# Latent attention heads of a diffusion backbone: scores turned to keys by queries, in a phase of their own

## The chip, the cores and the metric

The kernel runs on one core of one Trainium2 chip. The metric is the device time of one execution in microseconds (us); less is better. The core has a matmul engine (TensorE, PE in the profile, with its weight loads as PEld), a vector engine (DVE), a scalar engine (ACT), a general engine (POOL) and a queue that issues the transfers (SP). Each runs its own instructions strictly in the order in which they were written, and waits on semaphores for the others.

## The reference

A backbone of two layers works on 1024 latent tokens and 256 context tokens of width 1024. Layer 0 has two groups of attention heads side by side: four differential heads and eight latent heads (multi-head latent attention). Layer 1 is an mLSTM with a neighbourhood attention, and is not touched here. What the change touches is the attention of the latent heads:

```python
def softmax_attention(q, k, v, scale):
    def one(qb):
        s = jnp.einsum('bhqd,bhkd->bhqk', qb, k).astype(F32) * scale
        p = jax.nn.softmax(s, axis=-1).astype(v.dtype)
        return jnp.einsum('bhqk,bhkd->bhqd', p, v)
    return blocked_queries(one, q)
...
    oa = rms_norm(diff_attention(q1, q2, k1, k2, vd, lam), subln_g) * (1.0 - lam_init)
    ob = softmax_attention(qm, km, vm, MLA_SCALE)
    y = jnp.concatenate([from_heads(oa), from_heads(ob)], axis=-1) * jax.nn.silu(gate)
```

A latent head has 96 rows of queries and keys (64 plus 32 rotated ones) and 64 columns of values. All is in fp32. A latent query sees 1280 keys (1024 latent and 256 context tokens), a context query only the 256 context keys. A softmax is the same whatever is subtracted from all the scores of one query, so long as the exponentials stay in range.

## The kernel before

The kernel goes through stages: the conditioning and the input projection of layer 0 (to about 460 us in the profile), the attention of layer 0 (460 to 1006 us), its output projection, and layer 1. Only the attention stage concerns us.

**Units and tiles.** The stage has eight units: four `Differential` heads and four `Latent` units of two heads each. A unit works on ten tiles of 128 queries: eight latent ones with 1280 keys, and two context ones with 256. An fp32 operand is kept as two fp32r numbers, a high and a low part, so that one product of scores takes several quick passes: two in a differential head (L568, L569), three in a latent head (L720 high by high, L721 high by low, L722 low by high).

**One latent tile, one head** (`Latent.plan`): `cut` writes the scores, 128 queries by 1280 keys, in pieces of 512, 512 and 256 columns into one of two wide score buffers in PSUM (`s`, three banks each). `top` (DVE, L1151) takes the highest score of each query, `exps` (ACT, L1158) takes the exponentials and their sum, `inverse` (L733) and `scale` (POOL, L737) divide by the sum. Then `turned` transposes the ten 128 by 128 pieces on PE (L1175), since the product with the values needs the keys on the partitions; `moves` copies them out of the two small PSUM buffers `tp` (L518, on ACT or DVE), and `values` (L745) multiplies them with the values, the two heads of a unit on the two halves of the output's partitions. The values, the probabilities and the transposes are plain fp32; each such product stands as two instructions in the profile.

**A differential tile** is alike, with two scores, two exponentials and one combination of both (L588, DVE), ten transposes and ten products with the values (L599).

**Order.** A planner (`Plan`) takes all tasks of the stage with a cost each, and always emits next the task that could start earliest by these costs. So the order on each engine is fixed before the run. It was given the units in two streams: the tiles of the differential heads and the tiles of the latent units, one of the first to one of the second (`RATE = 1.0`), the differential ones eight tiles ahead (`LEAD = 8`). So the first differential head runs nearly alone, and then both kinds alternate.

**Loads.** Each stream has one set of buffers for queries, keys and values (pool `a0` for the differential units, `a1` for the latent ones). The loads of a stream's next unit (`load_scores`, `load_values`; L543 to L545 and L690 to L692, by the SP queue) can start only when its last scores have been taken by PE. A latent unit loads two times 2.0 MB of queries and keys (480 + 320 + 160 KB, high and low, for two heads), and 640 KB each of values and of the gate.

Of the kernel before, what the change touches and what calls it, by code (L numbers as in the profile page):

```python
# [49 lines left out]
NP = 5  # L50
# [87 lines left out]
def hybrid_kernel(ctx, tc, t, out, dbg=None):  # L138
# [352 lines left out]
    def on_vector(n):  # L491
        return 0.07 + n / 960
# [38 lines left out]
    class Differential(Unit):  # L531
        def __init__(self, h):
            self.h = h
            self.q, self.kh, self.kl = [None, None], [None, None], [None, None]
# [22 lines left out]
        def plan(self, tt):  # L557
# [53 lines left out]
            for b in range(2):  # L611
                last = None
                for n0, nn in key_cuts(w):
                    last = plan.add("P", 2 * nn / 2400, cut(b, n0, nn), [last or self.ready[b]], ["s"] if n0 == 0 else [],
                                    [f"dk{b}"] if tt == TILES - 1 and n0 + nn == w else [], rank=RD)
# [16 lines left out]
        def finish(self, t0, n, last):  # L632
# [42 lines left out]
            last = plan.add("V", 0.06 + on_vector(n * P), gated, [last], ["yd"], ["tp"] + (["dv"] if end else []))  # L675
# [4 lines left out]
    class Latent(Unit):  # L680
        def __init__(self, p):
            self.p, self.yy = p, {}
            self.qh, self.ql, self.kh, self.kl = [[None, None] for _ in range(4)]

        def load_scores(self, pool, a):
            p = self.p
            o = pool.tile([P, 4, NT], FR, name=f"o{a}")
            self.qh[a], self.ql[a], self.kh[a], self.kl[a] = [o[0:96, i, :] for i in range(4)]
            for i, (q, k) in enumerate(((self.qh, self.kh), (self.ql, self.kl))):
                dma(out=q[a].bitcast(F32), in_=s_mq[i][2 * p + a])  # L690
# [10 lines left out]
        def order(self):  # L701
            return [(tt, a) for tt in range(TILES) for a in range(2)]

        def plan(self, tt, a):
            k0, w = keys_of(tt)
            nch = w // P
            if a == 0:
                self.pair = []
            pair = self.pair
            x = {}  # L710
            pair.append(x)
            qsl = slice(tt * P, (tt + 1) * P)

            def cut(n0, nn):
                def emit(_):
                    if n0 == 0:
                        x["s"] = taken("s")
                    s = x["s"]
                    ks = slice(k0 * P + n0, k0 * P + n0 + nn)
                    T.matmul(s[:, n0:n0 + nn], self.qh[a][:, qsl], self.kh[a][:, ks], start=True, stop=False)  # L720
                    T.matmul(s[:, n0:n0 + nn], self.qh[a][:, qsl], self.kl[a][:, ks], start=False, stop=False)  # L721
                    T.matmul(s[:, n0:n0 + nn], self.ql[a][:, qsl], self.kh[a][:, ks], start=False, stop=True)  # L722
                return emit

            def top(_):
                x["m"] = highest(x["s"], w)

            def exps(_):
                x["p"], x["z"] = exponentials(x["s"], x["m"], w)
                given("s", x["s"])  # L730

            def inverse(_):
                V.reciprocal(out=x["z"], in_=x["z"])  # L733

            def scale(cs):
                def emit(_):
                    G.tensor_scalar(out=x["p"][:, cs], in0=x["p"][:, cs], scalar1=x["z"], scalar2=1.0,  # L737
                                    op0=ALU.mult, op1=ALU.mult)
                return emit

            def values(_):
                x["o"] = o = taken("tp")
                for c in range(nch):
                    for b in range(2):
                        T.matmul(o[64 * b:64 * b + 64, :P], self.v[:, k0 + c, b * 64:(b + 1) * 64], pair[b]["pt"][:, c, :],  # L745
                                 start=c == 0, stop=c == nch - 1)
                for y in pair:
                    given("pt", y["pt"])

            def gated(_):  # L750
                i = tt % 2
                if i == 0:
                    self.yy[tt // 2] = at.tile([P, 256], F32, name="yy", bufs=2)
                V.tensor_tensor(out=self.yy[tt // 2][:, i * P:(i + 1) * P], in0=x["o"][:, :P], in1=self.gate[:, qsl],
                                op=ALU.mult)
                given("tp", x["o"])

            def store(_):
                dma(out=s_y[4 + self.p, :, (tt - 1) * P:(tt + 1) * P], in_=self.yy[tt // 2])

            last = None
            for n0, nn in key_cuts(w):
                last = plan.add("P", 3 * nn / 2400, cut(n0, nn), [last or self.ready[a]], ["s"] if n0 == 0 else [],
                                [f"mk{a}"] if tt == TILES - 1 and n0 + nn == w else [], rank=RM)
            last = plan.add("V", on_vector(w), top, [last], rank=RANK)
            last = plan.add("A", on_scalar(w) + 0.1, exps, [last], ["p"], ["s"], rank=RANK)
            last = plan.add("V", 0.08, inverse, [last], rank=R1)
            done = [plan.add("G", on_pool(nn), scale(slice(n0, n0 + nn)), [last]) for n0, nn in pieces(w)]
            x["moved"] = turned(lambda: x["p"], x, w, done)
            if a:  # L770
                o = plan.add("P", 0.27 * nch, values, pair[0]["moved"] + x["moved"] + self.ready[2:], ["tp"], ["pt", "pt"])
# [1593 lines left out]
```

## Time and profile before

| | |
|---|---|
| median of 3 runs | 1916.51 us (1907.38 to 1920.92) |
| the profiled execution | 1925.9 us, its span 1923.8 us |
| mean granted PE clock of the span | 0.974 |
| PE busy | 1811.8 us, 94% of the span |
| DVE, ACT, POOL busy | 1083.7, 782.2, 527.2 us |
| attention stage | 460.6 to 1006.5 us, 546 us |

How to read it: a group is one line of the code on one engine with one form of operands; it shows how often it ran, its busy time together and the mean of one. Matmuls are pipelined, so the length of one is longer than the distance to the next; what a matmul costs PE is the distance between two starts. "PEclk" is the share of full speed at which the chip let PE run.

### The profile page before, as it was taken

Reading aid. Unit: us, or ns where it says so; the run is one execution under the profiler, and the core shown is the slowest. Engines: PE = TensorE matmul, PEld = TensorE weight load, DVE = VectorE, ACT = ScalarE, POOL = GpSimd, SP = SyncE. Lnnn points to the kernel's source line nnn. Section 1 sums busy time; section 2 is a strip of 40 time slices with the busy share of each in tenths; the row PEclk is TensorE's granted clock in tenths of the full one; section 3 lists DMA queues with packets and bytes.
Section 4 is the critical chain, followed back from the end, with each engine's and each line's share of the span. In section 5 each row is a group of like instructions: output and inputs, shape, how many; then the busy total and the mean of one; then the engine's idle time right before and its main releaser. Section 6 shows DMA issues by size and latency. Waiting matters only on the chain.

```text
span 1923.8 us, 33069 instructions
## 1 busy us (share of the span) xinstructions
PE 1811.8 (94%) x12493; PEld 1579.9 (82%) x12493; DVE 1083.7 (56%) x2273; ACT 782.2 (41%) x1622; POOL 527.2 (27%) x650
## 2 busy tenths in 40 slices
PE   7999999999989989899999989999998998998898
PEld 5898999887878778688878879788898877887786
DVE  2754124322867667567757863765766124667756
ACT  2311013433756656556653222324543223444521
POOL 1433124210133322223454422220111002223444
PEclk9999999999999999899999999999999999999999
DMA  9766524668330741830856432225442366677642
GB/s 285 238 206 203 169 76 129 184 192 200 74 86 15 163 107 22 167 92 13 215 165 224 142 138 77 78 74 194 152 136 76 107 191 173 167 188 194 180 159 88
DMA packets 242755, 276.17 MB, mean 144 GB/s; under 512 B 25170, under 2 KB 203294, under 8 KB 242598
## 3 DMA queue, kind: packets, MB, share of 16 engines
q1 hardware_dynamic: 242598, 274.07, 49.6%
q8 instruction: 99, 1.62, 0.3%
q14 instruction: 58, 0.48, 0.1%
HBM read 193.14 MB, written 87.16 MB: 146 GB/s over the span
## 4 chain that ended last, share of the span: by engine, by line
PE 62%; DMA 9%; DVE 5%; issue 2%; ACT 2%; SPq 2%; POOL 0%; DVEq 0%; POOLq 0%; ACTq 0%
PE mm L390 7%; PE mm L392 7%; PE mm L391 7%; PE tp L1175 4%; PE tp L745 4%; DMA o<-s_qk 3%; PE tp L599 3%; PE mm L1778 3%; PE mm L1779 3%; PE mm L1780 3%; PE s L569 2%; DMA o<-s_kr 2%; PE s L568 2%; PE s L720 2%; PE tp L2211 2%
## 5 line engine op out<-in xcount | busy, mean ns | idle before, releaser
L1151 DVE TENSOR_REDUCE nm<-s 128x1 f32<-128x1280 f32 (+1 forms) x160 | 202.9, 1274 | 105.1 <-PE s L569 71.5
L1158 ACT ACTIVATE p<-s,nm 128x1280 f32<-128x1280 f32 (+1 forms) x160 | 185.6, 1160 | 44.4 <-DVE nm L1151 31.7
L737 POOL TENSOR_SCALAR p<-p,zs 128x512 f32<-128x512 f32 (+1 forms) x208 | 128.4, 634 | 270.3 <-DVE zs L733 235.2
L518 ACT COPY pt<-tp 128x256 f32<-128x256 f32 x346 | 118.7, 375 | 113.2 <-PE tp L1175 106.5
L1175 PE MATMUL tp<-cst,p 128*128 128x128 f32 x1008 | 157.0, 279 | 3.8 <-DVE zs L733 1.4
L347 POOL TENSOR_TENSOR wlo<-raw,whi 128x1024 fp32r<-128x1024 f32 (+2 forms) x40 | 96.7, 2417 | 213.5 <-ACT whi L339 213.4
L1175 PEld LDWEIGHTS tp<-cst,p 128*128 128x128 f32 x1008 | 120.9, 143 | 34.3 <-issue 8.9
L390 PE MATMUL mm<-whi,hhi 128*128 128x256 f32 (+1 forms) x496 | 147.6, 298 | 0.5 <-DVE z L975 0.5
L392 PE MATMUL mm<-whi,hlo 128*128 128x256 f32 (+1 forms) x496 | 146.6, 296 | 0.2 <-DVE hlo L290 0.2
L391 PE MATMUL mm<-wlo,hhi 128*128 128x256 f32 (+1 forms) x496 | 146.4, 295 | 0.0
L339 ACT CAST whi<-raw 128x1024 fp32r<-128x1024 f32 (+2 forms) x54 | 55.9, 1036 | 178.4 <-DMA raw<-in_ev_w_in_dram 72.7
L2168 POOL TENSOR_SCALAR np<-np,nrz 128x640 f32<-128x640 f32 x64 | 52.1, 818 | 235.1 <-DVE nrz L2165 221.0
L568 PE MATMUL s<-o 128*128 128x512 f32 (+1 forms) x208 | 86.7, 419 | 16.4 <-DMA o<-s_qk 8.6
L518 DVE COPY pt<-tp 128x256 f32<-128x256 f32 x158 | 64.2, 421 | 66.8 <-ACT pt L518 57.8
L390 PEld LDWEIGHTS mm<-whi,hhi 128*128 128x128 f32 x496 | 94.6, 191 | 2.8 <-issue 1.7
L392 PEld LDWEIGHTS mm<-whi,hlo 128*128 128x128 f32 x496 | 94.5, 191 | 0.5 <-DVE hlo L290 0.4
L391 PEld LDWEIGHTS mm<-wlo,hhi 128*128 128x128 f32 x496 | 94.7, 191 | 0.2
L720 PE MATMUL s<-o 96*128 96x512 f32 (+1 forms) x208 | 87.8, 422 | 1.4 <-ACT p L1158 1.4
L599 PE MATMUL tp<-v,pt 128*128 128x128 f32 x672 | 85.1, 282 | 0.2
L745 PE MATMUL tp<-pt,v 128*64 128x128 f32 x1344 | 83.8, 279 | 0.4 <-ACT pt L518 0.2
L599 PEld LDWEIGHTS tp<-v,pt 128*128 128x128 f32 x672 | 80.7, 196 | 4.1 <-ACT pt L518 1.9
L721 PE MATMUL s<-o 96*128 96x512 f32 (+1 forms) x208 | 74.8, 360 | 9.4 <-DMA o<-s_kr 9.4
(451 smaller groups left out, 5049.2 us busy)
## 6 DMA issues: line engine op xcount, KB each, us to landing
adaw<-in_ada_w_dram SPq DMA_DIRECT2D x16, 1024.0 KB
raw<-in_od_w_in_dram SPq DMA_DIRECT2D x32, 512.0 KB
o<-s_qk SPq DMA_DIRECT2D x48, 320.0 KB
raw<-in_ev_w_in_dram SPq DMA_DIRECT2D x18, 512.0 KB
bt<-s_bt SPq DMA_DIRECT2D x16, 576.0 KB
adaw<-in_ada_w_dram SPq DMA_DIRECT2D x16, 512.0 KB
o<-s_mq SPq DMA_DIRECT2D x16, 480.0 KB
s_gate<-e SPq DMA_DIRECT2D x24, 256.0 KB
```

Source lines behind the costliest of these rows:

```text
L390: T.matmul(ps, ahi(k), bhi(k), start=k == k0, stop=False)
L391: T.matmul(ps, ahi(k), blo(k), start=False, stop=False)
L392: T.matmul(ps, alo(k), bhi(k), start=False, stop=k == nk - 1)
L518: copy_by(eng)(out=dst()[:, c0:c1, :], in_=bank()[:, c0 * P:c1 * P].rearrange("p (c q) -> p c q", q=P))
L568: T.matmul(s[:, n0:n0 + nn], ql, self.kh[b][:, ks], start=True, stop=False)
L599: T.matmul(o[:, :P], x["pt"][:, c, :], self.v[:, k0 + c, :], start=c == 0, stop=c == nch - 1)
L720: T.matmul(s[:, n0:n0 + nn], self.qh[a][:, qsl], self.kh[a][:, ks], start=True, stop=False)
L737: G.tensor_scalar(out=x["p"][:, cs], in0=x["p"][:, cs], scalar1=x["z"], scalar2=1.0, op0=ALU.mult, op1=ALU.mult)
L745: T.matmul(o[64 * b:64 * b + 64, :P], self.v[:, k0 + c, b * 64:(b + 1) * 64], pair[b]["pt"][:, c, :], start=c == 0, stop=c == nch - 1)
L1151: V.tensor_reduce(out=nm, in_=s[:, :w], axis=AX.X, op=ALU.max, negate=True)
L1158: S.activation(out=p[:, :w], in_=s[:, :w], func=AF.Exp, bias=nm, accum_out=z)
L1175: T.transpose(ps[:, c * P:(c + 1) * P], p()[:, (c0 + c) * P:(c0 + c + 1) * P], ident)
```

## The change

The differential heads come first, all four, and then the four latent units in a phase of their own (the two streams, `RATE` and `LEAD` are not used any more). The units alternate between the two sets of buffers (`place`), so a unit's loads can start when the unit before the last one has ended.

A latent unit works on groups of 512, 512 and 256 queries (`TG`), in two steps:

- `shifts`: for each head and each tile of 128 queries only the leading pass (high by high) is taken, into the wide buffer `s` (`rough`, L716); DVE takes the highest of each query with its sign turned (`top`, L724), four of them are transposed into one row (`turn`, L732), and ACT writes it as a 97th row under the low part of the queries (`row`, L737). The high part of the keys has a 97th row of ones, which POOL writes at each load (L692). The group after the current one has its shifts taken between the blocks of the current one.
- `scores`: one block is 128 keys by 512 queries (`block`, L763 to L765): three passes again, of which the third has 97 rows and so subtracts the shift. `exps` (L779) takes the exponential, which already has the keys on the partitions. `values` (L799) takes it as the moving operand, 64 rows of output for each head by 512 queries, for five chunks of keys at a time. The sums of the exponentials are added up chunk by chunk (`total`, L790, on DVE or POOL), one product with ones sums them over the partitions (`sums`, L807), `inverse` (L814) takes the reciprocal in two halves, and `gated` and `scaled` (L821, L825) apply the gate and the reciprocal.

One of the two wide buffers `s` is handed over to the blocks as three buffers `st` of one bank each (`banks`); the shifts have the other one alone. The ten wide tiles `p` and `pt` now hold the ten chunks of one group.

```diff
-            self.qh[a], self.ql[a], self.kh[a], self.kl[a] = [o[0:96, i, :] for i in range(4)]
+            self.qh[a], self.ql[a], self.kh[a], self.kl[a] = [o[:, i, :] for i in range(4)]
+            G.memset(self.kh[a][96:97, :].bitcast(F32), 1.0)
...
-        def plan(self, tt, a):
...
+            def rough(a, i, n0, nn):
...
+                    T.matmul(x["s", a, i][:, n0:n0 + nn], self.qh[a][0:96, (t0 + i) * P:(t0 + i + 1) * P],
+                             self.kh[a][0:96, k0 * P + n0:k0 * P + n0 + nn], start=True, stop=True)
...
+                    V.tensor_reduce(out=x["m", a][:, i:i + 1], in_=x["s", a, i][:, :w], axis=AX.X, op=ALU.max, negate=True)
+                    given("s", x["s", a, i])
...
+                        T.transpose(x["t", a][0:1, i * P:(i + 1) * P], x["m", a][:, i:i + 1], ident)
...
+                    S.copy(out=self.ql[a][96:97, t0 * P:(t0 + n) * P], in_=x["t", a][0:1, :n * P])
...
+                    T.matmul(st[:, :nq], self.kh[a][0:96, ks], self.qh[a][0:96, qs], start=True, stop=False)
+                    T.matmul(st[:, :nq], self.kl[a][0:96, ks], self.qh[a][0:96, qs], start=False, stop=False)
+                    T.matmul(st[:, :nq], self.kh[a][0:97, ks], self.ql[a][0:97, qs], start=False, stop=True)
...
+                    S.activation(out=flat(c)[:, 512 * a:512 * a + nq], in_=x["st", c, a][:, :nq], func=AF.Exp)
...
+                    e.tensor_tensor(out=acc, in0=before, in1=flat(c)[:, 512 * a:512 * a + nq], op=ALU.add)
...
+                            T.matmul(x["o"][64 * a:64 * a + 64, :nq], self.v[:, k0 + c, 64 * a:64 * a + 64],
+                                     flat(c)[:, 512 * a:512 * a + nq], start=c == 0, stop=c == nch - 1)
...
+                    T.matmul(x["z"][64 * a:64 * a + 64, :nq], ones[:, 0:64], x["acc"][:, a, :nq], start=True, stop=True)
...
-        steps = sorted([(RATE * n - LEAD, 0, n) for n in range(tiles)] + [(n, 1, n) for n in range(tiles)])
...
+        loaded(da[1])
+        for u in da:
+            for tt in range(TILES):
+                if tt == 4 and u.h:
+                    loaded(units[u.h + 1])
...
+        for i, (u, g) in enumerate(groups):
+            if g == 0 and u.p < 3:
+                loaded(mla[u.p + 1])
+            ahead = groups[i + 1][0].shifts(plan, groups[i + 1][1]) if i + 1 < len(groups) else []
+            steps = u.scores(plan, g)
```

In the whole program the latent heads have, before: 624 score passes, 672 transposes and 672 products with the values (1344 instructions). Now: 208 passes for the shifts (128 of 512 columns, 80 of 256), 528 passes in the blocks (480 of 512 columns, 48 of 256), 80 small transposes, 176 products with the values (160 of 512 columns, 16 of 256) and 24 with ones.

How the order on the engines changed, at three places. First PE before, in the middle of the stage, where a differential head (L568, L569, L599) and a latent unit (L720 to L722) alternate; `o` are queries and keys, `p` probabilities, `pt` their transposes:

```order
L720 MATMUL s_4839<-o_6652 128x512
L721 MATMUL s_4839<-o_6652 128x512
L722 MATMUL s_4839<-o_6652 128x512
L1175 MATMUL tp_4840<-cst,p_4842 128x128 x4
L720 MATMUL s_4839<-o_6652 128x512
L721 MATMUL s_4839<-o_6652 128x512
L722 MATMUL s_4839<-o_6652 128x512
L1175 MATMUL tp_4841<-cst,p_4842 128x128 x4
L720 MATMUL s_4839<-o_6652 128x256
L721 MATMUL s_4839<-o_6652 128x256
L722 MATMUL s_4839<-o_6652 128x256
L1175 MATMUL tp_4840<-cst,p_4842 128x128 x2
```

Of these rows the transposes have gone, and the three passes of scores stand in blocks of 512 queries. Now PE in the latent phase, at the change from the second latent unit (`o_6990`, `o_7046`) to the third (`o_7556`, `o_7585`): the last products with the values and the ones of the old unit, and the shifts of the new one.

```order
L799 MATMUL tp_4840<-p_4843,v 64x256 x2
L799 MATMUL tp_4840<-pt_4848,v 64x256 x2
L807 MATMUL tp_4841<-oo,cst 64x256 x2
L716 MATMUL s_4839<-o_7556 128x512 x2
L716 MATMUL s_4839<-o_7556 128x256
L716 MATMUL s_4839<-o_7556 128x512 x2
L716 MATMUL s_4839<-o_7556 128x256
L732 MATMUL tp_4841<-cst,nmx 1x128 x4
L716 MATMUL s_4839<-o_7585 128x512 x2
L716 MATMUL s_4839<-o_7585 128x256
L763 MATMUL s_4838<-o_7556 128x512
L764 MATMUL s_4838<-o_7556 128x512
```

Before, a latent score had the other stream's work and the other buffer beside it. Now all shifts go through the one buffer `s_4839`, and at a change of units three of them and the row's transposes stand behind each other with no other work between them.

Third DVE, before in the middle of the stage and now in the third latent unit:

```order
L1151 TENSOR_REDUCE nm<-s_4838 128x1
L588 SCALAR_TENSOR_TENSOR p_4844<-p_4843,ratio,p_4844 128x512
L1151 TENSOR_REDUCE nm<-s_4839 128x1
L733 RECIPROCAL zs<-zs 128x1
L588 SCALAR_TENSOR_TENSOR p_4844<-p_4843,ratio,p_4844 128x512
L588 SCALAR_TENSOR_TENSOR p_4844<-p_4843,ratio,p_4844 128x256
L518 COPY pt_4851<-tp_4841 128x256 x2
```

That was before; the same engine now:

```order
L790 TENSOR_TENSOR oo<-oo,pt_4847 128x512
L790 TENSOR_TENSOR oo<-oo,p_4843 128x512
L724 TENSOR_REDUCE nmx<-s_4839 128x1
L821 TENSOR_TENSOR yd<-tp_4841,gt 128x512
L724 TENSOR_REDUCE nmx<-s_4839 128x1
L814 RECIPROCAL rz<-tp_4840 128x256
L724 TENSOR_REDUCE nmx<-s_4839 128x1
L814 RECIPROCAL rz<-tp_4840 128x256
L724 TENSOR_REDUCE nmx<-s_4839 128x1
```

The copies of the transposes are gone from the latent heads; in their place DVE has 47 of the 144 additions of 512 columns (POOL has the other 97) and the wide reciprocals, and each of these stands ahead of a `top` that PE waits for.

More of the change, by code (lines that the diff above doesn't have):

```diff
@@ L736, in emit, with top @@
+                return emit
+            def top(a, i):
                 def emit(_):
-                    G.tensor_scalar(out=x["p"][:, cs], in0=x["p"][:, cs], scalar1=x["z"], scalar2=1.0,
-                                    op0=ALU.mult, op1=ALU.mult)
-                return emit
[L741 to L748, printed above, removed]
@@ L756, in gated, with scaled @@
                 given("tp", x["o"])
+            def scaled(_):
+                V.tensor_tensor(out=x["y"], in0=x["y"], in1=x["rz"][:, :nq], op=ALU.mult)
             def store(_):
[L759 to L771, printed above, removed]
-                last = plan.add("V", on_vector(P), gated, [o], [] if tt % 2 else ["yy"],
-                                ["tp"] + (["mv"] if tt == TILES - 1 else []), rank=R1)
-                if tt % 2:
-                    last = plan.add("D", 1.0, store, [last], [], ["yy"])
-                    if tt == 1:
-                        stored.append(last)
+                dma(out=s_y[4 + self.p, :, qs], in_=x["y"])
@@ L779, in hybrid_kernel @@
+            return [partial(step, c) for c in range(nch)]
     class Output:
@@ L1286, in hybrid_kernel @@
+        for i in range(2):
+            spread(plan, out0.load(i, lambda i=i: out0.y[i]), [*stored, w_half[0]])
         plan.run()
```

200 lines of the change are left out of this document (138 added, 62 removed).

## Prediction

> **What bounds the kernel now.** I read the page's engine table first, then the attention stage cut into stretches (span, then busy time and count for PE, PEld, DVE, ACT and POOL, then granted PE clock, DMA share, GB/s).
>
> ```profile
> 460.00:1006.00 546.00, 508.30 (x4107) 439.61 (x4105) 372.91 (x684) 340.55 (x795) 173.38 (x284) 0.96 0.43 105
> ...
> 476.00:507.00 31.00, 29.50 (x217) 26.67 (x217) 26.94 (x43) 24.18 (x59) 1.93 (x5) 1.00 0.31 76
> ...
> 560.00:650.00 90.00, 89.26 (x770) 78.70 (x768) 66.04 (x121) 60.20 (x148) 24.02 (x40) 1.00 0.23 58
> 650.00:700.00 50.00, 41.19 (x285) 34.53 (x282) 27.54 (x50) 25.61 (x56) 15.08 (x28) 0.90 0.86 197
> ...
> 750.00:850.00 100.00, 88.92 (x679) 76.17 (x679) 64.12 (x124) 57.82 (x139) 30.92 (x54) 0.91 0.60 131
> ```
>
> PE bounds the stage: where both kinds of head alternate undisturbed (560 to 650) it is busy 99% of the time. The stage still loses 37.7 us of PE idle time (546.0 less 508.3), and 4% of its clock. Two stretches lose most of it, 650 to 700 and 750 to 850, with the DMA engines at 86% and 60% and a clock of 0.90 and 0.91. The waits of PE in the stage (us in total, times, longest) say for what:
>
> ```profile
> PE s L721 <- DMA o<-s_kr: 9.4, 4, 5.6
> PE s L568 <- DMA o<-s_qk: 8.6, 5, 3.5
> PE s L568 <- ACT p L1158: 7.8, 10, 1.9
> PE s L569 <- DMA o<-s_qk: 6.0, 6, 1.2
> ```
>
> 24.0 us go to the loads of a next unit, which can't start before the last one's scores are done. Together with the clock, 0.10 of 50 and 0.09 of 100 us, these changes of units cost 38 us.
>
> **The price of a pass.** Starts of matmuls in an undisturbed stretch (start, length, name, count):
>
> ```profile
> 863.19 0.40 PE L720 MATMUL s<-o 96*128 96x512 f32 x1
> 863.42 0.40 PE L721 MATMUL s<-o 96*128 96x512 f32 x1
> ...
> 863.88 1.04 PE L1175 MATMUL tp<-cst,p 128*128 128x128 f32 x8
> 864.68 0.47 PE L720 MATMUL s<-o 96*128 96x512 f32 x1
> 864.99 0.39 PE L721 MATMUL s<-o 96*128 96x512 f32 x1
> ...
> 865.56 0.28 PE L721 MATMUL s<-o 96*128 96x256 f32 x1
> 865.68 0.28 PE L722 MATMUL s<-o 96*128 96x256 f32 x1
> ...
> 866.12 2.40 PE L745 MATMUL tp<-pt,v 128*64 128x128 f32 x40
> 868.45 0.50 PE L720 MATMUL s<-o 96*128 96x512 f32 x1
> 868.79 0.39 PE L721 MATMUL s<-o 96*128 96x512 f32 x1
> ```
>
> A pass of 512 columns costs 0.23 us (863.19 to 863.42, and three of them to 863.88), one of 256 columns 0.117 (865.56 to 865.68). Eight transposes take 0.80, and the pass behind them 0.31 instead of 0.23, so 0.11 each. Forty instructions with the values take 2.33 (866.12 to 868.45), 0.058 each, and the pass behind them 0.34, so a change from fp32 to fp32r costs 0.1.
>
> **Latent work on PE.** It loses 672 transposes, 73.9 us, and 1344 instructions with the values, 78.3. The scores stay at three passes, 116. It gains the shifts, 128 times 0.23 and 80 times 0.117, 38.8; 80 small transposes, 8.8. The new products with the values are 176, 352 instructions, and no row shows fp32 at 512 columns. The upper end is four times 0.058, 0.233 each. For the lower end: two overlapped instructions of 128 columns take 0.117, and a transpose of as many columns 0.10; if the 0.017 between them doesn't grow, a pair of 512 takes 0.417, 0.209 each. I take 0.222, between: 320 times that and 32 times 0.111, 74.6, and the 24 products with ones 8.9. So 268 us become 247, a gain of 21. That two heads overlap on the two halves of the output at wider columns too is shown elsewhere, with four products of 32 rows at 256 columns:
>
> ```profile
> L234 PE MATMUL mm<-adaw,sil 128*32 128x256 f32 x256 | 15.9, 382 | 0.0
> ```
>
> 0.062 us each, where one alone would take as long as 256 columns of a single pass, 0.117, at the least.
>
> **The differential heads alone.** They already ran alone at the start:
>
> ```profile
> 460.64 0.39 PE L568 MATMUL s<-o 128*128 128x512 f32 x1
> ...
> 464.99 0.55 PE L568 MATMUL s<-o 128*128 128x512 f32 x1 [1.87 <-ACT p L1158]
> 465.34 0.63 PE L569 MATMUL s<-o 128*128 128x512 f32 x1
> 465.77 0.63 PE L568 MATMUL s<-o 128*128 128x512 f32 x1
> ...
> 476.05 2.40 PE L599 MATMUL tp<-v,pt 128*128 128x128 f32 x20
> ...
> 493.21 0.50 PE L568 MATMUL s<-o 128*128 128x512 f32 x1 [1.44 <-ACT p L1158]
> 493.55 0.39 PE L569 MATMUL s<-o 128*128 128x512 f32 x1
> 493.77 0.39 PE L568 MATMUL s<-o 128*128 128x512 f32 x1
> ```
>
> ```profile
> L1158 ACT ACTIVATE p<-s,nm 128x1280 f32<-128x1280 f32 x11 | 14.7, 1334 | 1.3 <-DVE nm L1151 1.1
> L588 DVE SCALAR_TENSOR_TENSOR p<-p,ratio,p 128x512 f32<-128x512 f32 x10 | 7.4, 746 | 0.1
> ```
>
> In the 31 us from 476 to 507 there are 11 exponentials and 10 combinations, two of each to a tile, so about 5.25 tiles: 5.9 us each, with DVE at 87%. The start takes 15.4 us to the first product with values, of which some 8 were work (three tiles of scores at 2.3, ten transposes); 7 are lost. So the phase is 7, 32 tiles at 5.9 (189), eight context tiles at about 1.2 (four passes of 256, two transposes and four instructions with values by the prices above; 10) and 40 last transposes at 0.11 (4): 210 us. The loads hide under it: a unit has 50 us to bring in 5 MB, which at the 197 GB/s of the stretch above takes 26.
>
> **Waits of the latent phase.** Durations (busy, mean ns) in the stage, then two groups from layer 1, then POOL and DVE beside each other in the output projection:
>
> ```profile
> L1151 DVE TENSOR_REDUCE nm<-s 128x1 f32<-128x1280 f32 x128 | 190.0, 1488 | 103.6 <-PE s L569 70.3 <-PE s L722 31.9
> L1158 ACT ACTIVATE p<-s,nm 128x1280 f32<-128x1280 f32 x128 | 170.4, 1332 | 40.1 <-DVE nm L1151 28.9 <-DVE zs L733 9.0 <-DVE r L640 0.8
> ...
> L1158 ACT ACTIVATE p<-s,nm 128x256 f32<-128x256 f32 x32 | 15.2, 475 | 4.2 <-DVE nm L1151 2.8 <-DVE ratio L582 0.9
> ```
>
> ```profile
> L2054 DVE RECIPROCAL e<-e 128x128 f32<-128x128 f32 x32 | 28.5, 926 | 0.1
> ...
> L2061 POOL TENSOR_TENSOR e<-e,hv 128x512 f32<-128x512 f32 x8 | 10.3, 1282 | 19.1 <-DVE e L2057 14.5 <-DVE nrz L2165 4.6
> ```
>
> ```profile
> 1080.39 2.64 POOL L347 TENSOR_TENSOR gt<-yr,v 128x1024 fp32r<-128x1024 f32 x1 [5.77 <-ACT v L339]
> ```
>
> ```profile
> 1080.69 2.89 DVE L1336 SCALAR_TENSOR_TENSOR rr<-rr,gp 128x512 f32<-128x512 f32 x1
> ...
> 1086.27 0.69 DVE L1336 SCALAR_TENSOR_TENSOR rr<-rr,gp 128x512 f32<-128x512 f32 x1
> ```
>
> A group of 512 queries takes PE about 30 us. ACT has 20 exponentials of 512, 0.69 each between its two rows: 14 us, far below. POOL has 12 additions at 1.28, 15. DVE has eight `top` of 1.49, six additions at 0.69, 3.7 of reciprocals and 1.4 for gate and scale: 21. So PE stays the bound, and what counts is where it must wait in order.
>
> One place is each unit's start. A shift needs the one buffer back: 1.49 for `top` and about 0.2 for signals, 1.7. Three shifts and the transposes follow each other there, so two waits of 1.7, then 0.7 for the row (a copy on ACT near 0.5, signals) less the pass that stands between; the second head's row costs the same again once, 2.5. The last products of the old unit wait for an exponential of 256 (0.475 and signals) and two additions on POOL, 1.9 together. That is 8.5 idle.
>
> The clock comes on top: behind the idle 1.87 us above, passes start 0.43 apart instead of 0.23; behind 1.44 they don't. A unit's start idles more than half of several us, so I add 3 us of halved clock. The Trainium skill, "TensorE: Matmul & The Clock Gate", section "Why this matters for your kernels", halves the clock only after a gap of about 3 us; by that rule these 3 would be nothing and the sum 9 us less. The row at 464.99 speaks against it, and I keep them. So 11.5 for each of three starts, 6 for the first, which lies under the last differential tiles, and 4 at the end before the output projection: 45.
>
> Inside a group DVE puts reciprocals (1.85 for half a group) and additions ahead of a `top`; PE has two to four blocks, 1.4 to 2.8 us, between two shifts, so most of it hides. I take 1.5 us a group, 12, and 6 for some 60 changes to fp32r at 0.1.
>
> **The sum.** 210 + 247 + 45 + 12 + 6 = 520 us against 546: 26 us less. Other stages keep their instructions. The profiled execution took 1925.9 us (span 1923.8) and would take 1900; from the median of the runs, 1916.5 and 0.5% lower, 1890.
>
> **Rivals.**
>
> *The phase runs as smoothly as 560 to 650.* Starts and groups then cost 10 instead of 57, and the time is 1843. For it: in a group PE has 30 us of work and no other engine over 21. Against: there two score buffers and another stream filled the gaps. Chance 0.17.
>
> *The waits at the changes of units stay.* SP issues in order; if a next unit's loads stand behind a waiting store, the 38 us return: 1928. Against: a unit's loads are issued a whole unit ahead. Chance 0.12.
>
> *POOL blocks DVE, and DVE the shifts; the kernel gets slower.* The DVE instruction above takes 0.69 alone and 2.89 beside POOL's: it waits until POOL is done. In the latent phase POOL adds half of the time, and DVE's additions stand ahead of `top` in its queue. If each of the 64 wide shifts loses one POOL addition (1.28), that is 82 us, less the 12 already in: 1960. From 30 of 64 on nothing of the gain is left. Against: DVE has only 47 such additions, and PE has blocks in between. Chance 0.14. The Trainium skill, "SBUF — State Buffer", section "Who interferes with whom", states it as a rule: a DVE instruction with two SBUF inputs contends with a GpSimd one that reads SBUF, and the later blocks fully; the rows agree. It exempts reductions, as `top` is one, which only queue behind.
>
> *The two heads don't overlap at 512 columns.* The products with values and ones double, 83 more: 1973. Chance 0.03, by the row of L234.
>
> **The numbers.** The forecast has 0.54. Its own range is 1866 to 1914: 5 us for the price of the products, 15 for the starts (6 to 16 us each), 12 for the groups (0 to 3), not all at one end. About 1% is what can be told from no change, so "same" is 1897 to 1936. Faster: 0.17 for the smooth phase and 0.35 of the forecast, 0.52. Same: 0.19 of the forecast and 0.12 for the loads, 0.31. Slower: 0.14 and 0.03, 0.17. The range for 8 in 10 goes from about the smooth phase to two thirds of the blocked additions, 1845 to 1940, and leaves out the rest of both and the lost overlap.
>
> **What would show it.** Differential tiles 5.9 us apart with nothing else between them; no wait of PE for `o` loads; L799 at 0.209 to 0.233 us each; idle time of PE by L724 and L779 at the three changes of latent units, with a clock below 1.0 only there. Wrong if L716 waits inside groups, if L790 on DVE has a mean far over 0.7, or if L799 costs 0.4.

## The result and the profile after

The changed kernel takes 2105.27 us (median of 4 runs, 2102.94 to 2107.39) against 1916.91 for the kernel before (4 runs, 1907.38 to 1920.92). The ratio is 1.0994, with a 95% interval of 1.0956 to 1.1031: slower by a tenth, where 1.4% faster was forecast and the range ended at 1940. The profiled execution has a span of 2101.2 us against 1923.8.

The page of the changed kernel, its row for PE and the granted clock of PE in 40 equal slices of 52.5 us:

```profile
PE 1908.6 (91%) x11069; PEld 1540.6 (73%) x11069; DVE 1098.6 (52%) x2125; ACT 722.0 (34%) x1451; POOL 539.4 (26%) x553
...
PEclk9999999999999776665768899999999999999999
```

PE has 11069 products instead of 12493, and yet it is busy for 97 us longer (1811.8 before). The clock row says where: from the fourteenth slice, at 683 us, to the end of the twenty-third, at 1208, it is 0.5 to 0.8. That is the latent phase. The same in stretches, the differential phase and the latent phase (span, busy time and count for PE, PEld, DVE, ACT, POOL, then granted clock, DMA share, GB/s).

```profile
460.00:705.00 245.00, 214.42 (x1426) 188.98 (x1425) 198.32 (x343) 161.52 (x399) 37.09 (x66) 0.94 0.54 127
705.00:1187.00 482.00, 398.22 (x1267) 218.48 (x1266) 190.29 (x193) 119.93 (x226) 146.22 (x121) 0.71 0.20 55
```

The attention stage takes 727 us instead of 546. The differential phase was forecast at 210 and takes 245; the latent phase was forecast at 310 (247 of work, 63 of waits) and takes 482. Everything behind it takes 914 us against 918 before (the spans less 1187 and 1006).

Who waits in the latent phase, by the view of the waits of PE (us in total, times, longest):

```profile
PE s L763 <- ACT pt L779: 31.4, 48, 0.9
PE s L763 <- ACT p L779: 29.3, 44, 1.2
PE s L716 <- DVE nmx L724: 13.7, 12, 2.2
```

92 of the 176 blocks of scores wait for an exponential, 60.7 us together. No such wait was in the forecast: ACT has 119.9 us of work in 482, and the blocks have three banks to go on with. The sequence of PE and ACT shows how it comes about (start, length, engine, line, and in brackets the idle time before with its releaser):

```profile
722.65 0.63 PE L763 MATMUL s<-o 96*128 96x512 f32 x1
...
723.51 0.63 PE L765 MATMUL s<-o 97*128 97x512 f32 x1
723.93 0.63 PE L763 MATMUL s<-o 96*128 96x512 f32 x1
...
724.72 0.40 PE L765 MATMUL s<-o 97*128 97x512 f32 x1
...
725.16 0.60 ACT L779 ACTIVATE p<-s 128x512 f32<-128x512 f32 x1 [2.50 <-PE s L765]
725.81 0.50 PE L763 MATMUL s<-o 96*128 96x512 f32 x1 [0.69 <-ACT p L779]
...
726.38 0.40 PE L765 MATMUL s<-o 97*128 97x512 f32 x1
726.82 0.60 ACT L779 ACTIVATE pt<-s 128x512 f32<-128x512 f32 x1 [1.06 <-PE s L765]
727.47 0.50 PE L763 MATMUL s<-o 96*128 96x512 f32 x1 [0.69 <-ACT pt L779]
```

A first block ends at 724.1 (723.51 and 0.63), a second at 725.1. The exponential of the first begins at 725.16, a full microsecond after its own block and 0.04 us after the second. It ends at 725.76, and the third block begins at 725.81, although a third bank should have been free for it. From there block and exponential alternate: 726.38 and 0.40 make 726.78, the exponential of the second block starts at 726.82, the fourth block 0.05 us after its end. Three banks, and never a block and an exponential at the same time: in the whole phase no row of L779 overlaps one of L763 to L765.

The program as built says why. For the first blocks of the phase, in its order: which columns of which tile each instruction takes, what count it waits for, and by how much it raises its engine's count.

```
L765 PE   s0_4838 from column 0     raises nothing
L765 PE   s0_4838 from column 512   raises PE by 6, to 4109
L779 ACT  s0_4838 from column 0     waits for PE 4109
L779 ACT  s0_4838 from column 512   raises ACT by 2, to 491
L763 PE   s0_4838 from column 1024  waits for ACT 491
L765 PE   s0_4838 from column 0     raises PE by 6, to 4122
L779 ACT  s0_4838 from column 1024  waits for PE 4122
```

The exponential of columns 0 to 511 waits for the count that the block in columns 512 to 1023 raises, and the exponential from column 1024 for a block written behind it, from column 0. The block in column 1024 waits for the exponential of other columns, from 512. The three `st` are slices of one tile, and here each reader of the tile waits for every write to it that stands ahead in the program, whatever its columns, and each writer for every reader. The planner, which counted three buffers, puts the next block ahead of the exponential (it could start earlier), and so makes the exponential wait for it. This reading is theory A below. Theory B takes the shifts for the cause (one buffer, a maximum of 1.5 us each, and a clock that falls with it), theory C is the prediction's third rival: POOL's additions hold DVE, and DVE the shifts.

### The profile page after: what moved, and what is told of

Read it like the earlier page. It is cut to its first block, busy times and chain, and to the rows that moved or that the text cites. A ratio compares the mean times of both kernels' runs of the same rounds, so it can differ in the third digit from the quotient of the medians.

```text
span 2101.2 us, 29560 instructions
## 1 busy us (share of the span) xinstructions
PE 1908.6 (91%) x11069; PEld 1540.6 (73%) x11069; DVE 1098.6 (52%) x2125; ACT 722.0 (34%) x1451; POOL 539.4 (26%) x553
## 3 DMA queue, kind: packets, MB, share of 16 engines
q8 instruction: 88, 1.44, 0.3%
## 4 chain that ended last, share of the span: by engine, by line
PE 58%; DVE 10%; ACT 6%; DMA 4%; issue 3%; POOL 1%; SPq 1%; ACTq 0%; DVEq 0%; POOLq 0%
PE mm L390 5%; PE mm L392 5%; PE mm L391 5%; PE tp L799 4%; PE s L763 4%; PE tp L599 3%; PE s L765 3%; PE s L764 3%; PE mm L1873 2%; PE mm L1874 2%; PE mm L1875 2%; ACT p L779 2%; ACT pt L779 2%; PE tp L1254 2%; PE s L716 2%
## 5 line engine op out<-in xcount | busy, mean ns | idle before, releaser
L724 DVE TENSOR_REDUCE nmx<-s 128x1 f32<-128x1280 f32 (+1 forms) x80 | 101.3, 1273 | 146.3 <-PE s L716 146.0
L763 PE MATMUL s<-o 96*128 96x512 f32 (+1 forms) x176 | 104.7, 595 | 61.8 <-ACT pt L779 31.4
L1230 DVE TENSOR_REDUCE nm<-s 128x1 f32<-128x1280 f32 (+1 forms) x80 | 101.5, 1275 | 66.5 <-PE s L569 62.9
L763 PEld LDWEIGHTS s<-o 96*128 96x128 f32 x176 | 44.3, 252 | 124.5 <-ACT p L779 56.9
L779 ACT ACTIVATE pt<-s 128x512 f32<-128x512 f32 (+1 forms) x88 | 50.2, 576 | 161.1 <-PE s L765 161.1
L568 PE MATMUL s<-o 128*128 128x512 f32 (+1 forms) x208 | 85.2, 414 | 20.9 <-ACT p L1237 20.6
L1237 ACT ACTIVATE p<-s,nm 128x1280 f32<-128x1280 f32 (+1 forms) x80 | 92.8, 1161 | 30.6 <-DVE nm L1230 25.8
L779 ACT ACTIVATE p<-s 128x512 f32<-128x512 f32 (+1 forms) x88 | 50.1, 576 | 145.5 <-PE s L765 145.5
L765 PE MATMUL s<-o 97*128 97x512 f32 (+1 forms) x176 | 91.0, 517 | 0.0
L764 PE MATMUL s<-o 96*128 96x512 f32 (+1 forms) x176 | 90.3, 513 | 0.0
L716 PE MATMUL s<-o 96*128 96x512 f32 (+1 forms) x208 | 75.5, 470 | 13.7 <-DVE nmx L724 13.7
L599 PE MATMUL tp<-v,pt 128*128 128x128 f32 x672 | 84.7, 283 | 0.1
L599 PEld LDWEIGHTS tp<-v,pt 128*128 128x128 f32 x672 | 82.5, 199 | 1.9 <-ACT pt L518 0.3
```

The lines of the kernel that those rows point to most:

```text
L599: T.matmul(o[:, :P], x["pt"][:, c, :], self.v[:, k0 + c, :], start=c == 0, stop=c == nch - 1)
L716: T.matmul(x["s", a, i][:, n0:n0 + nn], self.qh[a][0:96, (t0 + i) * P:(t0 + i + 1) * P], self.kh[a][0:96, k0 * P + n0:k0 * P + n0 + nn], s ...
L724: V.tensor_reduce(out=x["m", a][:, i:i + 1], in_=x["s", a, i][:, :w], axis=AX.X, op=ALU.max, negate=True)
L763: T.matmul(st[:, :nq], self.kh[a][0:96, ks], self.qh[a][0:96, qs], start=True, stop=False)
L764: T.matmul(st[:, :nq], self.kl[a][0:96, ks], self.qh[a][0:96, qs], start=False, stop=False)
L765: T.matmul(st[:, :nq], self.kh[a][0:97, ks], self.ql[a][0:97, qs], start=False, stop=True)
```

## The experiments

**Three tiles.** In the handover of the buffer, the tile `s0` is released and three tiles take its place. The order of the instructions and the arithmetic stay.

```diff
-            s_ = taken("s")
-            for i in range(3):
-                given("st", s_[:, i * 512:(i + 1) * 512])
+            assert taken("s") is s0
+            ps0.close()
+            three = ps3.enter_context(space(name="ps3", bufs=1, space=PSUM))
+            for i in range(3):
+                given("st", three.tile([P, 512], F32, name=f"st{i}"))
```

> The three banks that the score blocks take in turn are allocated as three tiles instead of as three slices of the tile s0; nothing else changes, the arithmetic least of all. Theory A (false waits): in the changed kernel every exponential starts 0.04 us after the end of the NEXT block's third pass and the block after that waits for this exponential, because the waits are kept per tile; with three tiles each exponential follows its own block, the 61 us that PE waits by L763 go to under 10, the granted clock of the latent phase rises from 0.71 to 0.9 or more, and the span falls from 2101 to 1920 to 1960. Theory B (the shifts break the flow and let the clock fall): at most the 61 us go, the clock of the phase stays below 0.8 and the span above 2030. Theory C (additions on POOL hold DVE, and DVE the shifts): within 15 us of 2101.

Measured: 1929.49 us (4 runs), 1.0058 of the kernel before (1.0041 to 1.0074); span 1928.7. The latent phase by stretch, by the waits of PE, and in sequence:

```profile
705.00:1010.00 305.00, 279.73 (x1250) 175.16 (x1249) 198.93 (x189) 123.15 (x223) 150.45 (x121) 0.93 0.32 87
```

```profile
PE s L716 <- DVE nmx L724: 12.4, 13, 1.9
PE tp L732 <- DVE nmx L724: 7.7, 8, 1.9
PE tp L807 <- DVE rz L814: 4.2, 4, 1.5
PE st L763 <- DVE nmx L724: 0.6, 1, 0.6
PE st L763 <- ACT p L779: 0.2, 1, 0.2
```

```profile
738.09 0.40 PE L765 MATMUL st<-o 97*128 97x512 f32 x1
738.33 0.40 PE L763 MATMUL st<-o 96*128 96x512 f32 x1
738.53 0.60 ACT L779 ACTIVATE p<-st 128x512 f32<-128x512 f32 x1 [0.55 <-PE st L765]
738.56 0.40 PE L764 MATMUL st<-o 96*128 96x512 f32 x1
738.79 0.40 PE L765 MATMUL st<-o 97*128 97x512 f32 x1
```

The exponential at 738.53 follows its own block (738.49), while the next block runs. Of 60.7 us of waits for exponentials 0.2 are left, and the phase falls by 177 us, to 305. Theory A holds in each of its numbers, B and C gave over 2030 and about 2101. Of the 177 us only 59 are idle time (482 less 398.2 against 305 less 279.7); the other 118 are busy time of the same products. Two things make them up, by an estimate from these rows. The clock was 0.71 instead of 0.93, and 279.7 us of work at the one would take 366 at the other: some 87. And a block behind a wait stands alone, so that the start of its first pass and the end of its last are covered by nothing: it takes 0.97 us (725.81 to 726.78) where a block in the flow takes 0.70 (738.33 to 739.03), which at 92 places makes 25. So the waits cost their idle time and the broken blocks, and the clock that falls with them costs more than the idle time.

**The order alone.** The new order of units with the class `Latent` of the kernel before: scores by query tile, transposes, POOL's scaling.

```diff
-        groups = [(u, g) for u in mla for g in range(len(TG))]
...
+        for u in mla:
+            for tt in range(TILES):
+                for a in range(2):
+                    u.plan(tt, a)
```

> The new order with the old method: the differential heads in a phase of their own, then the latent heads alone with their scores by query tile, transposes and POOL scaling as before. If the new order is harmless (A): the differential phase takes 240 to 250 us as in the changed kernel, the latent phase its 268 us of PE work plus the 14 per cent of waits that the differential phase shows, about 310, together 555 against 546, so a span of 1915 to 1950. If a phase of one kind of head alone is what lets the clock fall (B'): the latent phase shows a clock under 0.85, and the span is above 2000.

Measured: 1923.76 us (8 runs), 1.0017 of the kernel before (1.0000 to 1.0034).

```profile
460.00:705.00 245.00, 214.10 (x1455) 188.72 (x1455) 199.44 (x347) 163.49 (x406) 32.49 (x62) 0.96 0.56 129
705.00:1010.00 305.00, 293.85 (x2688) 249.35 (x2687) 186.46 (x366) 170.16 (x364) 144.22 (x225) 1.00 0.33 89
```

The order of units neither helps nor harms: what the differential phase loses, the old latent method, alone, makes good. It keeps PE busy 96% of its phase at a clock of 1.00. So a phase of one kind of head is not what lets the clock fall, and the new method with its three tiles (305 us too) had by then won nothing over the old one: less work (280 us of PE against 294), but more waits (25 us against 11).

**No shifts.** The rough products, the maxima and the transposed rows are left out of the changed kernel, which keeps its slices of one tile.

```diff
+            G.memset(self.ql[a][96:97, :].bitcast(F32), 0.0)
...
-            return [partial(step, a, i) for a in range(2) for i in range(n)]
+            return []
```

> The shifts are left out: no rough product, no maximum, no turn, a row of zeros in the place of the shift, and the exponential takes 0.001 of the score so that it stays finite; the three banks stay slices of one tile. So the result leaves the true scores out, and only the time is of use. Theory A (false waits): PE loses the shifts' work (87 us busy by L716 in the phase at its low clock, 20 by L732) and their 19 us of waits, but block and exponential still alternate: waits of about 0.69 us stay before nearly every block outside the values, more than 61 us of them in all, the clock of the phase stays at 0.75 or below, the span is 1960 to 2020. Theory B (the shifts break the flow): waits by L763 under 20 us, clock 0.9 or more, span about 1870.

Measured: 2052.98 us (1 run), span 2051.2. Of the waits and the phase (lines behind the edit stand one further down in this kernel):

```profile
PE s L764 <- ACT pt L780: 45.7, 65, 1.2
PE s L764 <- ACT p L780: 43.8, 61, 1.2
```

```profile
705.00:1140.00 435.00, 344.25 (x999) 161.27 (x998) 131.34 (x161) 110.08 (x199) 89.98 (x78) 0.69 0.24 64
```

Without any shift the waits for exponentials grow, to 89.5 us at 126 blocks, and the clock is as low as before. Theory B falls. The span lies above the 1960 to 2020 that theory A gave. A shift between two blocks had given the exponentials time, which the expectation left out: in the changed kernel three passes of L716 at 728.45 run beside two exponentials, and the block behind them, at 729.83, has no wait.

**All additions on DVE.**

```diff
-                        x["sum"][a] = plan.add("VG", (on_vector(nq), 0.1 + nq / 440), total(c, a),
+                        x["sum"][a] = plan.add("V", on_vector(nq), total(c, a),
```

> All additions of exponentials on DVE, none on POOL. Theory C (POOL holds DVE, and DVE the shifts): the waits of PE by L716 and L763 fall by half or more and the span by 60 us or more. Theory A (false waits) and theory B (shifts): POOL is off the path, the span stays within 20 us of 2101.

Measured: 2106.69 us (1 run), span 2104.9; the waits by L763 are 57.3 us (29.5 and 27.8), those by L716 13.9. POOL's part is off the path, and theory C falls. The changed kernel's own rows had said so (groups of the latent phase: busy, mean ns of one, idle before):

```profile
L790 DVE TENSOR_TENSOR oo<-oo,p 128x512 f32<-128x512 f32 x20 | 13.9, 701 | 20.2 <-ACT p L779 20.1
```

**Shifts one group earlier.** Three tiles, and what is left of the waits in the first experiment are shifts at the changes of latent units, where the context group (2 key tiles) has to hide eight shifts of the next unit. They move under the group before.

```diff
-            ahead = groups[i + 1][0].shifts(plan, groups[i + 1][1]) if i + 1 < len(groups) else []
+            ahead = [f for v, h in groups[i + 1:i + 1 + (1, 2, 0)[g]] for f in v.shifts(plan, h)]
```

> Three tiles as in the first experiment, and the shifts of a latent unit's first group are planned one group earlier: under the second group of the unit before, beside those of the context group, no longer under the context group, which has 2 key tiles instead of 10 to hide them. In the first experiment PE waits 20 us for shifts (12.4 by L716, 7.7 by L732), mostly at the three changes of units, with a clock of 0.67 to 0.72 there. Theory A (the rest of the loss is these starts): the waits by L716 and L732 fall under 10 us, the clock of the latent phase from 0.93 to 0.97 or more, the span from 1929 to 1895 to 1915. Rival (DVE, with twelve maxima instead of four under the second group, becomes late there): waits of the same size move into the second groups, 1920 to 1940.

Measured: 1906.58 us (7 runs), 0.9939 of the kernel before (0.9910 to 0.9967); span 1902.1.

```profile
PE s L716 <- DVE nmx L724: 5.3, 7, 2.0
PE tp L732 <- DVE nmx L724: 3.3, 5, 1.2
```

```profile
705.00:985.00 280.00, 268.69 (x1257) 166.84 (x1256) 204.33 (x183) 123.07 (x223) 165.13 (x129) 0.99 0.35 94
```

The waits for shifts fall from 20.1 to 8.6 us, the clock rises from 0.93 to 0.99, the phase falls by 25 us. This version beats both kernels, the one before by a small 0.6%, the changed one by 9%.

**Two banks, and a filled gap.** Two kernels on the question of the clock. In the first, the blocks get two of the three banks, as slices of one tile, and the third bank lies idle; in the second, two more passes are put ahead of each block, into the idle bank, which nobody reads.

```diff
+                    for _ in range(2):
+                        T.matmul(spare["fill"][0][:, :nq], self.kh[a][0:96, ks], self.qh[a][0:96, qs], start=True, stop=True)
```

> As the changed kernel, but only two of the three banks are given to the score blocks, again as slices of one tile; the third bank lies idle. It is the base for the next run. Theory A (false waits): block and exponential alternate already in the changed kernel, so the third bank was of no use and the span stays within 25 us of 2101. If the third bank did help: 2150 or more.

> As the run before, with two more passes of the block's first product ahead of each block, into the third bank, which nobody reads or waits for: 352 passes, 320 of 512 columns at 0.23 us and 32 of 256 at 0.117, 77 us of added PE work at full clock; they stand where PE waits for the exponential. Clock by activity: the gaps are filled, the granted clock of the latent phase rises from about 0.7 to 0.9 or more, and the span falls by 50 us or more, to 2050 or less, though PE does more work. Rival (the clock falls for another reason, as the kind of product or the neighbours on the chip): the clock stays at 0.7, a filling pass takes 0.43, the two 0.86 for a gap of 0.69, and the span rises to 2110 to 2160.

Measured, each in 1 run: two banks 2040.65 us, span 2038.9; with the filling passes 2048.82, span 2047.1. The latent phase of the one, with its waits and one gap of its sequence, then of the other:

```profile
705.00:1123.00 418.00, 343.20 (x1258) 197.15 (x1257) 192.89 (x189) 116.03 (x218) 148.24 (x123) 0.82 0.23 63
...
PE two L763 <- ACT pt L779: 44.8, 47, 1.2
PE two L763 <- ACT p L779: 15.2, 19, 1.2
...
862.68 0.50 PE L763 MATMUL two<-o 96*128 96x512 f32 x1 [1.23 <-ACT pt L779]
```

```profile
705.00:1127.00 422.00, 375.19 (x1645) 236.60 (x1645) 195.25 (x194) 118.08 (x226) 149.28 (x123) 0.97 0.24 65
```

Both expectations of a time were missed; the second kernel lies under its 2050 only because its base was faster than expected. With a bank less the kernel is 62 us faster. PE waits as long for exponentials (44.8 and 15.2 us, 60.0 against 60.7), but the planner now more often puts two blocks and then their two exponentials. So the same idle time comes as 66 gaps instead of 92, and 35 of them instead of 2 are of 1 us or more (1.23 behind two blocks), between longer bursts, and the clock is 0.82 instead of 0.71. That the grouping of the gaps makes this difference is read from these two runs and not tested by itself. The filling passes raise the clock from 0.82 to 0.97, as expected of a clock that follows what PE does, and the 77 us of work that they add lengthen the one run by 8 us, which is less than the runs of the kernel before differ by (1909 to 1925). But they don't make the kernel faster: the waits for exponentials fall only to 33.5 us, since a gap of 1.23 holds more than the two passes and other blocks had no gap to fill.

**The differential phase: less combination, and context tiles in between.** Two tries at the 35 us that this phase takes above its forecast. In the first, built on the three tiles, DVE combines only the first 512 keys of each tile (the rest is left out):

```diff
+                    if cs.start == 0:
                         V.scalar_tensor_tensor(out=p1, in0=p2, scalar=x["ratio"], in1=p1, op0=ALU.mult, op1=ALU.add)
```

> Three tiles as in the first experiment; of the combination of the two softmaxes of the differential heads (L588) only the first 512 keys are done, so the result leaves the rest out. That takes 1.25 us a tile from DVE in the differential phase (0.75 and 0.5), 40 us over 32 tiles. Theory D1 (the phase takes 245 us instead of 210 since DVE, busy for 6.2 us a tile, is what its queue order makes the others wait for): the phase falls to 205 to 220. Theory D2 (it is the cycle of two score buffers through PE, maximum and exponential, which keeps its length): it stays at 235 or more.

Measured: 1922.53 us (1 run), span 1920.8; the first shift of the latent phase starts at 694.2 instead of 704.0 us, so the differential phase gave back 10 of the 40 us that DVE lost. From 460 that is 234 us: theory D1 (205 to 220) falls, and the 235 of D2 is met to within 1. The products with the values of the first head, in the changed kernel and in this one:

```profile
481.54 2.39 PE L599 MATMUL tp<-v,pt 128*128 128x128 f32 x20
487.20 2.39 PE L599 MATMUL tp<-v,pt 128*128 128x128 f32 x20
```

```profile
478.83 2.39 PE L600 MATMUL tp<-v,pt 128*128 128x128 f32 x20
484.51 2.39 PE L600 MATMUL tp<-v,pt 128*128 128x128 f32 x20
```

A tile takes 5.66 us in the one and 5.68 in the other. That is PE's own work by the prediction's prices: four times 0.577 of scores, ten transposes of 0.11 and 2.33 of values make 5.7. So where the phase runs evenly PE bounds it and DVE has room, and the cycle of two buffers that D2 names is not what sets the even pace.

In the second, built on the shifts ahead, the two context tiles of a head stand between its full tiles instead of behind them (their release of buffers moves with them):

```diff
-            for tt in range(TILES):
+            for tt in (0, 1, 2, 3, 8, 4, 5, 9, 6, 7):
```

> The run with the shifts ahead (1906.6 us), and the two context tiles of each differential head no longer last but between its full tiles (order 0 1 2 3 8 4 5 9 6 7). The work is the same. In the changed kernel the maxima of the context tiles to the first full maximum of the next head take 6.5, 12.9 and 6.5 us at the three changes of heads and about 7 at the end, 33 where 10 were priced. Theory E1 (context tiles in a row at the end of a head, with waits for exponentials and combinations that are too short to hide, lengthen the phase): between full tiles they are hidden, the differential phase falls from 245 to 222 to 235, the span from 1902 to 1878 to 1893. Theory E2 (the planned order of heads two to four is uneven for other reasons): the phase stays at 240 or more, the span at 1895 or more.

Measured: 1914.54 us (10 runs), 0.9980 of the kernel before (0.9968 to 0.9992), and slower than the 1906.58 it was built on. The first shift starts at 709.6 instead of 704.0. Theory E1 falls: the context tiles cost more among the full ones. The waits of PE in the differential phase of the changed kernel, largest first, point to the score buffers, of which a differential head has two and a tile needs both:

```profile
PE s L568 <- ACT p L1237: 20.6, 16, 2.8
PE tp L1254 <- DVE p L588: 8.3, 13, 1.6
```

The first head takes from 462 to 513 us by its maxima, the others 60 to 65 each. Why the planned order keeps PE fed in the first head and not in the later ones has not been settled.

## Why the prediction was wrong

**The step that failed first** stands in "Waits of the latent phase": ACT has 14 us of exponentials in a group of 30, "far below", and "So PE stays the bound, and what counts is where it must wait in order". It took the three banks for three buffers, because the planner counts three, and compared only the engines' totals. In the program they are one tile, and block and exponential exclude each other: 60.7 us of waits by L763, a term that the sum has at nothing. This step is worth 177 of the 203 us between the forecast of the profiled execution (1900) and what it took (2103 with what lies around the span). None of the three signs of being wrong pointed to it: L716 waits at the starts of units more than in groups, L790 on DVE has its 0.70, L799 its price. But one of the signs of being right failed, and in this direction: waits by L779 and a clock below 1.0 were to show only at the three changes of units, and they fill the whole phase. The prediction had the code line that cuts the tile into slices before it, and the built program with its waits; the counts would have told.

**The clock** is the second half of the same error. The prediction had 3 us of half clock for each start of a unit, and read from the rows that an idle 1.87 us halves the clock and 1.44 doesn't. In the latent phase PE waits 115 times, 83 us in all, the longest 2.2 us and only four of them above 1.3, and the clock is 0.71 over 482 us: many gaps of 0.7 do it too. Of the 160 blocks of 512 columns 91 have their last two passes 0.43 apart and 67 have 0.23; with three tiles it is 11 and 147. The profile before had shown this already, within 10 us of the row that the prediction read: after waits of 1.22 and 0.35, with transposes between them, passes are 0.43 apart again (474.35 to 474.78).

```profile
470.36 0.50 PE L568 MATMUL s<-o 128*128 128x512 f32 x1 [1.22 <-ACT p L1158]
...
471.90 0.94 PE L1175 MATMUL tp<-cst,p 128*128 128x128 f32 x4 [0.35 <-DVE p L588]
...
474.35 0.63 PE L569 MATMUL s<-o 128*128 128x512 f32 x1
474.78 0.63 PE L568 MATMUL s<-o 128*128 128x512 f32 x1
475.20 0.55 PE L569 MATMUL s<-o 128*128 128x512 f32 x1
```

The Trainium skill, "TensorE: Matmul & The Clock Gate", has both rules: the section that the prediction cited, of a gap of some 3 us, and the section "A second HAM failure mode: psum-queue depth-cycling", where short idle times between groups of products that go through the banks of PSUM in turn make the clock go up and down. The traces agree with the second, by the two groups of blocks above, and not with the first, since no gap was longer than 2.2 us. The second gives no size; here it was some 87 us, by the estimate above.

**The differential phase** was forecast at 210 us from 31 smooth us of the first head, and took 245. The even pace was right (5.66 against 5.9 us). What it missed are 30.6 us in which PE is idle (245 less 214.4), with a clock of 0.94: the later heads are not like the first. That the latent tiles had filled these gaps before the change is likely, and not tested. The prediction allowed 7.

**What was right.** The prices: four instructions with the values at 512 columns in 0.86 us, 0.215 each, between the 0.209 and 0.233 that were given, so the two heads overlap:

```profile
745.55 1.02 PE L799 MATMUL tp<-p,v 128*64 128x512 f32 x4
746.41 1.02 PE L799 MATMUL tp<-pt,v 128*64 128x512 f32 x4
747.27 1.02 PE L799 MATMUL tp<-p,v 128*64 128x512 f32 x4
```

A pass of 97 rows takes 0.23 to 0.24 us, as one with 96 does. The waits for `o` loads are gone from the list, so that rival fell. With the false waits taken away, the latent phase takes 305 us where 310 were forecast, and its waits stand where they were put, at the starts of units: when the shifts move away from there the phase falls by 25. That 305 lies so close to 310 is partly luck: PE is idle for 25 us, where the terms of the sum hold 47.5 (8.5 at three starts, 6, 4 and 12 in the groups), and busy for 280, where they hold 262 (247, 9 of halved clock and 6).

**The rivals.** The smooth phase did not come about even in the best version. POOL did not block DVE here, where DVE had 60% of its time free; with the shifts ahead DVE's additions take 1.0 us instead of 0.70 (group of the latent phase), which fits the mechanism without proving it, but PE's waits for all shifts together are 8.6 us:

```profile
L790 DVE TENSOR_TENSOR oo<-oo,p 128x512 f32<-128x512 f32 x17 | 16.9, 995 | 4.0 <-ACT p L779 3.5
```

The rival that came true, a wait for a buffer that is free, was not among them. And of the 26 us of gain that were forecast the best version that was found has 12 (1906.6 against 1918.9 beside it).

## What to carry to other kernels

A buffer is what the waits are kept for, not what the planner counts: when one tile is cut into slices for several stages, read in the built program which count the first reader waits for, or give each slice a tile of its own. Compare the engines' totals only after that; an engine with a quarter of the work can still stand in every step of a chain. And price a short wait of PE by what it does to the clock as well: here 59 us more of gaps, nearly all under 1.3 us, brought another 118 us of longer products, some 87 of them by the clock.

## What the runs showed of the hardware

The granted clock of PE fell without any long pause: no gap in the changed latent phase was longer than 2.2 us. In the latent phases of these runs (idle share of PE, clock): 4% at 0.99 and 1.00, 8% at 0.93, 11% at 0.97 with the filling passes, 17% at 0.71 and 0.69, 18% at 0.82, 21% at 0.69. The idle share alone doesn't decide it, as the two runs with 60 us of the same wait and 0.71 and 0.82 show. Nor is a high clock enough: 77 us of products that nobody needs, put into the gaps, raised the clock from 0.82 to 0.97, and the kernel did not get faster (2048.82 us after 2040.65, one run each).
